# Row pitch in HBM: loads of 13,152 columns instead of 13,184 in a streaming Lp-pool kernel

## The chip, the cores and the metric

The kernel runs on one core of one Trainium2 chip. The metric is the device time of a run in microseconds, lower is better. Each quoted time is a median of several runs of the same kernel; all timed runs of this study were in the fast state (the one run of experiment e8 has an unknown state, because a single run has nothing to be compared with). A profile is one further execution.

## The reference

An Lp pool over windows of four with p = 2: for each group of four neighbouring values the root of the mean of their squares.

```python
x: float32 [32, 256, 4096], p = 2.0, kernel_size = 4
for i in range(1024):
    window = np.abs(x[:, :, 4*i:4*i+4]) ** p
    result[:, :, i] = np.mean(window, axis=-1) ** (1.0 / p)     # [32, 256, 1024]
```

134.2 MB come in and 33.6 MB go out. Windows never cross a row, so the kernel may treat x as one flat array.

## The kernel before

The flat array is cut into blocks of 128 rows, one row per partition of SBUF, the core's on-chip memory; HBM is the main memory that x and the result lie in. Two loads make a group: a block whose rows are two load widths long, and each load takes half of every row. So the row pitch in HBM is twice the load width, and the store's pitch is a quarter of that.

```python
W, O_W = 13184, 6592
X_SLOTS, O_SLOTS = 3, 2                       # three input buffers, two output buffers
slots = [[(W, [W])]] * 17 + [[(W, [6592, 6592])]]
slots += [[(6592, [6592]), (6592, [6592])], [(6592, [6592]), (4216, [2112, 2104])]]
ODD = 840                                     # the remainder, done first as 30 rows of 3584
groups = [2] * 9 + [3, 1]                     # loads to a group
late = {7, 8, 9, 10}                          # groups whose stores are issued after all loads
...
def block(flat, g, div):                      # group g of x (div = 1) or of the output (div = 4)
    at, width = sum(columns[:g]) * P // div, columns[g] * P // div
    return flat[at:at + width].rearrange("(p w) -> p w", p=P)

def load(i):
    ...
    nc.sync.dma_start(out=v, in_=block(xf, g, 1)[:, src:src + w])
...
def store(g, queue):
    stores[g] = queue.dma_start(out=block(of, g, k), in_=ots[g])
...
for i in range(n):                            # (cut) per load
    while ahead < n and loads[ahead][0] < s + X_SLOTS:
        load(ahead)                           # a load waits until its buffer's sums are done
        ahead += 1
    for step in chunks:
        nc.scalar.activation(out=v, in_=v, func=Act.Square)     # ScalarE, in place
        total_sum(ots[g][...], v, i)          # VectorE: a reduce over 4, or two adds (last 7 loads)
        while pending and pending[0][0] <= done - LAG:
            root(...)                         # ScalarE: Sqrt, then the group's store
for g in sorted(late):
    store(g, nc.sync)
```

## Time and profile before

| | before |
|---|---|
| time, median of 6 runs | 394.19 us (394.0 to 395.52) |
| span of the profiled run | 392.4 us |
| bytes moved | 167.77 MB, 428 GB/s over the span |
| busy: DMA engines / ScalarE / VectorE | 99.3% / 71% / 68% |
| load packet of 52,736 bytes: minimum / median | 1947 / 1947 ns |

The first row to read is the DMA share, because no compute engine is near full. The profile's lines for this table stand in the prediction below. A "packet" is one row of one partition; the 16 DMA engines have 16 of them in flight for 373 of the 392.4 us. Packet durations in this document come from the trace's records of single packets, of which the page shows only sums.

### The profile page before, as it was taken

Reading aid. Unit: us, or ns where it says so; the run is one execution under the profiler, and the core shown is the slowest. Engines: PE = TensorE matmul, PEld = TensorE weight load, DVE = VectorE, ACT = ScalarE, POOL = GpSimd, SP = SyncE. Lnnn points to the kernel's source line nnn. Section 1 sums busy time; section 2 is a strip of 40 time slices with the busy share of each in tenths; the row PEclk is TensorE's granted clock in tenths of the full one; section 3 lists DMA queues with packets and bytes.
Section 4 is the critical chain, followed back from the end, with each engine's and each line's share of the span. In section 5 each row is a group of like instructions: output and inputs, shape, how many; then the busy total and the mean of one; then the engine's idle time right before and its main releaser. Section 6 shows DMA issues by size and latency. Waiting matters only on the chain.

```text
span 392.4 us, 183 instructions
## 1 busy us (share of the span) xinstructions
DVE 268.5 (68%) x35; ACT 280.2 (71%) x39; POOL 0.2 (0%) x4
## 2 busy tenths in 40 slices
DVE  4307898885769476948693769396928690989481
ACT  1085879919990899099909990998099919999991
POOL 0000000000000000000000000000000000000000
DMA  8999999999999998999999999999999999999997
GB/s 318 425 441 430 446 441 441 411 435 470 430 398 430 473 430 387 430 473 430 411 441 438 430 473 425 392 430 430 430 435 452 446 430 446 409 430 416 446 430 321
DMA packets 4842, 167.77 MB, mean 428 GB/s; under 512 B 558, under 2 KB 558, under 8 KB 716
## 3 DMA queue, kind: packets, MB, share of 16 engines
q1 hardware_dynamic: 3789, 144.04, 85.3%
q10 hardware_dynamic: 1053, 23.73, 14.0%
HBM read 134.22 MB, written 33.55 MB: 428 GB/s over the span
## 4 chain that ended last, share of the span: by engine, by line
DMA 47%; ACT 34%; DVE 16%; SPq 0%; ACTq 0%; issue 0%
DMA xt<-in_x_dram 47%; ACT xt L162 28%; DVE ot L110 14%; ACT ot L101 6%; DVE xt L121 1%; DVE xt L123 1%; ACT xt L101 1%; ACTq L98 0%; SPq L81 0%; SPq L131 0%
## 5 line engine op out<-in xcount | busy, mean ns | idle before, releaser
L162 ACT ACTIVATE xt<-xt 128x13184 f32<-128x13184 f32 (+3 forms) x24 | 222.2, 9272 | 91.4 <-DMA xt<-in_x_dram 89.8
L110 DVE TENSOR_REDUCE ot<-xt 128x3296 f32<-128x13184 f32 x15 | 208.3, 13886 | 88.6 <-ACT xt L162 88.6
L101 ACT ACTIVATE ot<-ot 128x6592 f32<-128x6592 f32 x9 | 51.1, 5681 | 0.0
L121 DVE TENSOR_TENSOR xt<-xt 128x3296 f32<-128x3296 f32 (+3 forms) x9 | 34.5, 3836 | 22.5 <-ACT xt L162 22.2
L123 DVE TENSOR_TENSOR ot<-xt 128x3296 f32<-128x3296 f32 (+1 forms) x4 | 10.9, 2734 | 0.1
L142 ACT ACTIVATE ot<-ot 30x896 f32<-30x896 f32 x1 | 0.9, 948 | 10.9 <-DVE ot L138 10.9
L101 ACT ACTIVATE xt<-xt 128x3296 f32<-128x3296 f32 (+3 forms) x4 | 5.8, 1449 | 2.3 <-DVE xt L123 2.3
L136 DVE TENSOR_TENSOR ot<-ot 30x3584 f32<-30x3584 f32 x1 | 3.9, 3879 | 5.1 <-DMA ot<-in_x_dram 5.1
L123 DVE TENSOR_TENSOR xt<-xt 128x1648 f32<-128x1648 f32 (+2 forms) x5 | 7.0, 1407 | 0.2
L138 DVE TENSOR_REDUCE ot<-ot 30x896 f32<-30x3584 f32 x1 | 3.9, 3874 | 0.0
L142 ACT ACT_TABLE_LOAD x1 | 1.3, 1283 | 0.7 <-PEq L195 0.7
L195 POOL MEMSET const-bfloat16-1.0<- 128x1 bf16 x1 | 0.1, 101 | 0.0
L195 POOL MEMSET const-uint8-127<- 128x1 uint8 x1 | 0.1, 101 | 0.0
L195 POOL MEMSET const-float32-0.0<- 128x1 f32 x1 | 0.1, 98 | 0.2 <-issue 0.2
L195 POOL MEMSET const-float32-1.0<- 128x1 f32 x1 | 0.1, 98 | 0.0
## 6 DMA issues: line engine op xcount, KB each, us to landing
xt<-in_x_dram SPq DMA_DIRECT2D x18, 6592.0 KB, 31.3
out_dram<-ot ACTq DMA_DIRECT2D x7, 3296.0 KB, 27.0
xt<-in_x_dram SPq DMA_DIRECT2D x3, 3296.0 KB, 24.2
out_dram<-ot SPq DMA_DIRECT2D x2, 3296.0 KB, 26.2
out_dram<-xt SPq DMA_DIRECT2D x1, 2472.0 KB, 9.2
xt<-in_x_dram SPq DMA_DIRECT2D x1, 2108.0 KB, 23.7
out_dram<-xt SPq DMA_DIRECT2D x1, 527.0 KB, 5.9
ot<-in_x_dram SPq DMA_DIRECT2D x1, 420.0 KB, 4.3
```

The costliest lines, as they stand in the source:

```text
L101: r = nc.scalar.activation(out=o, in_=o, func=Act.Sqrt, scale=1.0 / k)
L110: r = nc.vector.tensor_reduce(out=o, in_=v.rearrange("p (n j) -> p n j", j=k), axis=mybir.AxisListType.X, op=add,)
L121: r = nc.vector.tensor_tensor(out=h, in0=q[:, :, 0:2], in1=q[:, :, 2:4], op=add)
L123: r = nc.vector.tensor_tensor(out=o, in0=h[:, :, 0], in1=h[:, :, 1], op=add)
L136: nc.vector.tensor_tensor(out=t, in0=t, in1=t, op=mybir.AluOpType.mult)
L138: nc.vector.tensor_reduce(out=o, in_=t.rearrange("p (n j) -> p n j", j=k), axis=mybir.AxisListType.X, op=mybir.AluOpType.add,)
L142: nc.scalar.activation(out=o, in_=o, func=Act.Sqrt, scale=1.0 / k)
L162: r = nc.scalar.activation(out=v, in_=v, func=Act.Square)
L195: nc = _bacc.Bacc("TRN2", target_bir_lowering=False, num_devices=1)
```

## The change

The intent: with rows of 105,472 bytes, rows four apart lie at the same place modulo 4 KB, since four rows are 103 x 4096 bytes. With 105,216 bytes they are 1 KB apart modulo 4 KB, which should spread the reads of the DMA engines in HBM.

```diff
-    W, O_W = 13184, 6592
+    W, O_W = 13152, 6576
-    slots = [[(W, [W])]] * 17 + [[(W, [6592, 6592])]]
-    slots += [[(6592, [6592]), (6592, [6592])], [(6592, [6592]), (4216, [2112, 2104])]]
+    slots = [[(W, [W])]] * 17 + [[(W, [6576, 6576])]]
+    slots += [[(6576, [6576]), (6576, [6576])], [(6576, [6576]), (4840, [3232, 1608])]]
-    in_x = {9: (2, 0), 10: (2, 4944)}
-    FINE, ENDS, LAG = {21}, {19, 20}, 1
+    in_x = {9: (2, 0), 10: (2, 4932)}
+    FINE, ENDS, LAGS = {21}, {19, 20}, {}
+    ON_DVE = set()
...
+            if (i, c) in ON_DVE:          # the set is empty: never taken
+                r = nc.vector.tensor_tensor(out=v, in0=v, in1=v, op=mybir.AluOpType.mult)
...
-            while pending and pending[0][0] <= done - LAG:
+            while pending and pending[0][0] <= done - LAGS.get(pending[0][1], 1):   # always 1
```

The last load grows from 4216 to 4840 columns, since it takes what the others leave.

More of the change, by code (lines that the diff above doesn't have):

```diff
@@ L161 @@
             v = xs[i][:, c:c + step]
-            r = nc.scalar.activation(out=v, in_=v, func=Act.Square)
-            follows(r, by_act[:-1])
-            by_act.append(r)
+            if (i, c) in ON_DVE:
+                r = nc.vector.tensor_tensor(out=v, in0=v, in1=v, op=mybir.AluOpType.mult)
+                follows(r, sums[:-1])
+            else:
+                r = nc.scalar.activation(out=v, in_=v, func=Act.Square)
+                follows(r, by_act[:-1])
+                by_act.append(r)
             total_sum(ots[g][:, summed:summed + step // k], v, i)
-            while pending and pending[0][0] <= done - LAG:
+            while pending and pending[0][0] <= done - LAGS.get(pending[0][1], 1):
                 root(*pending.pop(0)[1:])
```

## The prediction

> **What bounds the kernel now.** I read the page's slices first, because the kernel has no TensorE work and moves 167.8 MB.
>
> ```profile
> span 392.4 us, 183 instructions
> DVE 268.5 (68%) x35; ACT 280.2 (71%) x39; POOL 0.2 (0%) x4
> DMA  8999999999999998999999999999999999999997
> GB/s 318 425 441 430 446 441 441 411 435 470 430 398 430 473 430 387 430 473 430 411 441 438 430 473 425 392 430 430 430 435 452 446 430 446 409 430 416 446 430 321
> q1 hardware_dynamic: 3789, 144.04, 85.3%
> q10 hardware_dynamic: 1053, 23.73, 14.0%
> ```
>
> The compute engines are busy about 70% of the span, the DMA engines 85.3 + 14.0 = 99.3%. The rate wobbles by slice only because packets are long and are counted at their start. Wider stretches (length; DVE, ACT and POOL busy; clock; DMA share; GB/s) take the wobble away:
>
> ```profile
> 2.00:20.00 18.00, 7.75 (x2) 0.96 (x2) 0.00 (x0) 1.00 1.03 421
> 20.00:376.00 356.00, 253.42 (x28) 270.69 (x32) 0.00 (x0) 1.00 1.00 432
> 376.00:391.00 15.00, 7.28 (x6) 7.32 (x6) 0.00 (x0) 1.00 0.94 403
> ```
>
> From 20 to 376 us no DMA engine has time left. The chain of waits gives ScalarE and VectorE half of the path, which misleads here: the loads' queue waits for VectorE to free a slot, but it still has work queued.
>
> ```profile
> SPq L81 <- DVE ot L110: 301.6, 15, 43.2
> ...
> xt<-in_x_dram SPq DMA_DIRECT2D x18, 6592.0 KB, 31.3
> ```
>
> A 6.75 MB load needs 15.6 us at 432 GB/s, but takes 31.3 us from issue to landing: some 15 us of other traffic lies ahead of or between its packets. The issue therefore comes early enough.
>
> The question is then whether the engines move bytes as fast as they can, or whether their packets are drawn out by HBM, which is what the change wants to cure. I took the single packet records of the trace. Load packets of 52,736 bytes (one row of one partition; 2304 of them) take 1947 ns in the minimum, 1947 in the median, 1952 in the 90th percentile. The 1536 packets of 26,368 bytes (stores, and three half loads) take 978 in minimum and median. Two sizes give a line: (52,736 - 26,368) / (1947 - 978) = 27.21 bytes per ns and engine, plus 978 - 969 = 9 ns a packet. All the time above each size's median is 1.17 us per engine over the whole span, 0.54 of it in the first 20 us. Sum of the records by engine: first packet at 1.74 us, last end at 391.0 us[...]. So the 392.4 us are 1.74 us of start, 167.77 MB / 16 / 27.21 = 385.4 us of bytes, 4284 data packets / 16 x 9 ns = 2.4 us, 0.3 us of four-byte semaphore packets, 1.2 us of slow packets (sum 389.3), and 1.4 us of end.
>
> [...]
>
> **The change part by part.**
>
> Addresses. A group of two loads is one block of 128 rows of 2 x 13,184 x 4 = 105,472 bytes. Four rows are 421,888 = 103 x 4096[...]. With 13,152, four rows are 420,864 = 102.75 x 4096[...]. The kernel before holds its own control: the three half loads 18 to 20 form a group with rows of 79,104 bytes, four of which are 77.25 x 4096, also 1 KB apart, and stores of 26,368-byte rows are 1 KB apart too (25.75 x 4096). Both run at the same 978 ns, 8.6 ns above bytes / 27.2; the loads with equal addresses are 8.2 ns above. The spread buys nothing measurable there. Upper bound of what it can take away: the 1.17 us of slow packets. About 0.45 us of these are the first packets, drawn out while 16 engines start together, with the small first load of 30 partitions under way, which the change leaves; so I credit 0.3 us.
>
> Bytes and packets. The total is the same, to the byte: 32 columns fewer in 18 loads and 16 in each of three are 624 columns, and the last load grows from 4216 to 4840. The count of loads and stores stays, so 4284 data packets stay. A load packet becomes 52,608 / 27.21 + 9 = 1942 ns, a store packet 26,304 / 27.21 + 9 = 976 ns; the sums over bytes are equal. Change: 0.
>
> Alignment. 52,608 is 205.5 x 256, so each second load of a pair starts 128 bytes off; output rows of 26,304 bytes are 102.75 x 256.[...] But the 19,776-byte rows of group 9's store are 77.25 x 256 already, and take 735 ns where the line gives 736.[...]
>
> Compute. ScalarE squares 13,184 columns in 11.19 us and 6592 in 5.68, so 0.835 ns a column and 0.18 us fixed; VectorE's 13.89 us for a reduce shrinks by the same 0.24%. No instruction is added or removed. The squares on VectorE and the variable lag are switched off (an empty set, and a default of 1), so the order on every engine is unchanged. All of it lies beside the DMA.
>
> The tail. From 340.2 us ScalarE works without a pause of note until 385.6, so it could set the end:
>
> ```profile
> 373.92 2.95 ACT L101 ACTIVATE xt<-xt 128x3296 f32<-128x3296 f32 x1
> 376.78 1.95 ACT L162 ACTIVATE xt<-xt 128x2112 f32<-128x2112 f32 x1
> 379.51 1.58 ACT L101 ACTIVATE xt<-xt 128x1648 f32<-128x1648 f32 x1 [0.78 <-DVE xt L123]
> 381.11 4.88 SPq L98 DMA_DIRECT2D out_dram<-xt  x2
> ...
> out_dram<-xt SPq DMA_DIRECT2D x1, 2472.0 KB, 9.2
> ```
>
> Group 9's store is issued at 381.1 and lands 9.2 us later, while its 2.53 MB need 5.8 us at 432 GB/s: it stands 3.4 us behind the stores of groups 7 and 8. That is the slack of this chain. With the change load 17 lands some 0.7 us earlier (18 x 32 columns x 512 bytes = 0.29 MB at 432), seven squares and roots are 0.013 us shorter each, and the first chunk of the last load grows from 2112 to 3232 columns (2.88 us for 1.95, in place of the 0.78 us wait): 0.2 us later. Group 9's store comes about 0.6 us earlier. The last chunk falls to 1608 columns, its square to 1.52 us and the last roots to 0.85 and 0.52, so that the last store is issued near 384.1 instead of 385.6. It carries 0.62 MB instead of 0.54, taken from the stores before it. The queue empties at the same byte count: 0, with more slack.
>
> Sum: -0.3 + 0.3 + 0 + 0 = 0. The three runs before had 394.0, 395.49 and 395.52; their scatter is larger than anything in the sum. I put the new median between, at 394.9.
>
> **The rivals.** (a) The equal addresses do cost, in a way that packets hide. For it: 16 first packets at 2.2 to 2.9 us, and some 50 slow ones around 70 and 304 us just after a store was issued. Against it: their sum[...]. It would give 393.6 to 394.5, and cannot give more than 1.2 us. (b) The broken 256-byte alignment costs on both sides[...]. Against it: the 19,776-byte stores. (c) The tail turns bound to ScalarE: the larger first chunk would have to delay the store by 3.4 us more; it delays it by 0.2. Otherwise 396. (d) Smaller loads run the queue dry: impossible to see in a 0.24% change against 15 us queued ahead.
>
> **Range and chances.** A: 1.2 us down from the fastest seen before is 392.8[...]. The 2% lines are at 387.6 and 403.4. 387.6 less 1.8 us (394.2 for the profiled run, less its span) and 3.1 us of start and end leaves 382.7 us, less than the 385.4 us of bytes alone at 27.21[...]. Slower needs a new conflict of the spread addresses, which the control inside the trace speaks against. So 0.01, 0.97, 0.02.
>
> **What would show it.** Right: load packets near 1942 ns and store packets near 976, the share at 99%, 432 GB/s in the middle, the last store issued earlier but landed at the same time. If the first packets at 2 to 3 us fall to 1942, (a) is right in kind. If second loads or stores are over 10 ns above the line, (b). If the DMA share from 376 us on falls under 0.9, (c). Wrong outright: a middle rate above 435 or under 425 GB/s.

The sum came to 0: 0.3 us credited for the spread of addresses, 0.3 us charged for the lost alignment, 0 for compute and 0 for the tail. The charge, the upper bound of rival (b) and the upper end of the range, B, were worked out from a cost of a start off 256 bytes that was not shown; the charge stands in the line of the sum. 27.2 bytes per ns is, in the prediction or in an expectation, the measured 27.21, rounded.

## The result

394.49 us median of 6 runs (393.85 to 395.58), against 394.19 of before: the ratio is 1.0001, 95% interval 0.9977 to 1.0026, so the same. Here and below a ratio is the mean time of one kernel's runs over the mean of the other's runs of the same rounds, so it is not quite the ratio of the quoted medians.

The page of the changed kernel: its span, compute engines, the DMA's busy tenths and GB/s in 40 slices, and the two DMA queues (packets, MB, share).

```profile
span 392.3 us, 183 instructions
DVE 268.4 (68%) x35; ACT 280.2 (71%) x39; POOL 0.2 (0%) x4
DMA  8999999999989999999999999999999899999997
GB/s 307 433 436 429 445 445 461 394 434 469 434 386 429 472 429 413 461 413 429 429 429 429 429 472 429 429 432 459 429 440 429 386 432 469 405 443 417 444 432 321
q1 hardware_dynamic: 3789, 144.10, 85.3%
q10 hardware_dynamic: 1053, 23.68, 14.0%
```

Packets and shares are the same; 0.06 MB moved from the store queue to the load queue, because the earlier stores shrank. The three stretches of the changed kernel (length; DVE, ACT and POOL busy; clock; DMA share; GB/s):

```profile
2.00:20.00 18.00, 7.75 (x2) 0.96 (x2) 0.00 (x0) 1.00 0.99 407
20.00:376.00 356.00, 253.95 (x28) 271.19 (x33) 0.00 (x0) 1.00 1.00 433
376.00:391.00 15.00, 6.70 (x6) 6.83 (x5) 0.00 (x0) 1.00 0.96 406
```

The middle runs at 433 GB/s against 432. The 407 against 421 at the start is only where long packets happen to begin: the slow packets of that stretch cost 0.59 us per engine, against 0.53 before.

The load queue's wait for VectorE, from the changed kernel's waits, and the DMA table's time from issue to landing:

```profile
SPq L82 <- DVE ot L111: 300.7, 15, 43.3
...
xt<-in_x_dram SPq DMA_DIRECT2D x18, 6576.0 KB, 31.2
```

Both stand as before: long waits, and a load still finds some 15 us of traffic ahead of it, so the queue doesn't run dry, as the prediction's rival (d) would have it. The end of the changed kernel, from its timeline (start, duration; neighbours are merged, so the last line holds the stores of groups 9 and 10), and the landing time of group 9's store:

```profile
372.78 2.94 ACT L102 ACTIVATE xt<-xt 128x3288 f32<-128x3288 f32 x1
375.63 2.88 ACT L167 ACTIVATE xt<-xt 128x3232 f32<-128x3232 f32 x1
378.42 1.56 ACT L102 ACTIVATE xt<-xt 128x1644 f32<-128x1644 f32 x1
380.00 3.98 SPq L99 DMA_DIRECT2D out_dram<-xt  x2
...
out_dram<-xt SPq DMA_DIRECT2D x1, 2466.0 KB, 9.9
```

Group 9's store is issued 1.1 us earlier than before (380.00 against 381.11), takes 0.7 us longer to land, and the last packet ends at 390.9 us against 391.0. What compute gained, the queue took back. By packet: 52,608-byte loads have a minimum and a median of 1942 ns, 26,304-byte stores and half loads 975; the 90th percentile of the loads is 1942 too.

### The profile page after: what moved, and what is told of

The parts are those of the page before. It is cut to its first block, busy times and chain, and to the rows that moved or that the text cites. A ratio compares the mean times of both kernels' runs of the same rounds, so it can differ in the third digit from the quotient of the medians.

```text
span 392.3 us, 183 instructions
## 1 busy us (share of the span) xinstructions
DVE 268.4 (68%) x35; ACT 280.2 (71%) x39; POOL 0.2 (0%) x4
## 4 chain that ended last, share of the span: by engine, by line
DMA 47%; ACT 34%; DVE 15%; SPq 0%; ACTq 0%; issue 0%
DMA xt<-in_x_dram 47%; ACT xt L167 28%; DVE ot L111 14%; ACT ot L102 6%; ACT xt L102 1%; DVE xt L122 1%; DVE xt L124 0%; ACTq L99 0%; SPq L82 0%; SPq L132 0%
## 5 line engine op out<-in xcount | busy, mean ns | idle before, releaser
L167 ACT ACTIVATE xt<-xt 128x13152 f32<-128x13152 f32 (+3 forms) x24 | 222.2, 9272 | 90.9 <-DMA xt<-in_x_dram 89.2
L111 DVE TENSOR_REDUCE ot<-xt 128x3288 f32<-128x13152 f32 x15 | 207.8, 13853 | 88.2 <-ACT xt L167 88.2
L102 ACT ACTIVATE ot<-ot 128x6576 f32<-128x6576 f32 x9 | 51.0, 5669 | 0.0
L122 DVE TENSOR_TENSOR xt<-xt 128x3288 f32<-128x3288 f32 (+3 forms) x9 | 34.8, 3863 | 21.0 <-ACT xt L167 20.7
L124 DVE TENSOR_TENSOR ot<-xt 128x3288 f32<-128x3288 f32 (+1 forms) x4 | 10.9, 2726 | 0.1
L124 DVE TENSOR_TENSOR xt<-xt 128x1644 f32<-128x1644 f32 (+2 forms) x5 | 7.2, 1439 | 0.2
L102 ACT ACTIVATE xt<-xt 128x3288 f32<-128x3288 f32 (+3 forms) x4 | 5.9, 1479 | 0.8 <-DVE xt L124 0.8
```

The source lines that it names most:

```text
L102: r = nc.scalar.activation(out=o, in_=o, func=Act.Sqrt, scale=1.0 / k)
L111: r = nc.vector.tensor_reduce(out=o, in_=v.rearrange("p (n j) -> p n j", j=k), axis=mybir.AxisListType.X, op=add,)
L122: r = nc.vector.tensor_tensor(out=h, in0=q[:, :, 0:2], in1=q[:, :, 2:4], op=add)
L124: r = nc.vector.tensor_tensor(out=o, in0=h[:, :, 0], in1=h[:, :, 1], op=add)
L167: r = nc.scalar.activation(out=v, in_=v, func=Act.Square)
```

## The experiments

Theory: each DMA engine moves a packet in bytes / 27.21 + 9 ns, whatever the HBM address, so the time is set by bytes. Rivals: (a) the addresses matter but something hides it; (b) lost alignment eats a gain; (c) ScalarE's tail sets the end; and a fourth, from the page's chain: compute holds half the path. The runs were sent three times, four kernels each, and each time beside runs of the kernel before on the same chip: medians 394.42, 394.45 and 394.37 us. "Excess" is the time of load packets above their fast duration, summed and divided by 16 engines, in one profile.

### e1: the new kernel with the old row pitch

```diff
-        nc.sync.dma_start(out=v, in_=block(xf, g, 1)[:, src:src + w])
+        if g < 9:
+            first = sum(columns[:g]) * P + src
+            rows = xf[first:first + P * 26368].rearrange("(p w) -> p w", p=P)
+            nc.sync.dma_start(out=v, in_=rows[:, 0:w])
+        else:
+            nc.sync.dma_start(out=v, in_=block(xf, g, 1)[:, src:src + w])
```

> The changed kernel, but the loads of groups 0 to 8 read rows at the old pitch of 105,472 bytes[...], so only HBM read addresses differ; wrong result on purpose. Theory ([...]addresses modulo 4 KB don't matter): load packets stay at a median of 1942 ns, ratio to the kernel before 1.000 within 0.003, 394 to 395.5 us. Rival a (equal addresses cost, hidden in the changed kernel by a loss elsewhere): packets or first packets longer, 1 to 4 us slower than the changed kernel.

394.35 us, ratio 0.9989 (0.9973 to 1.0006); wrong result as intended. Load packets have a median and a 90th percentile of 1942 ns, and the excess is 1.0 us (0.8 in the changed kernel). With the addresses alone put back no loss is seen, so rival (a) fails as far as these runs can tell: the interval leaves room for about 1 us (0.3%), not for more.

### e2: the old kernel with the new row pitch

The same edit in the kernel before, with `P * 26304` in place of 26368.

> The kernel before with its own sizes, tail and 256-byte-aligned rows, but loads of groups 0 to 8 read rows at the new pitch of 105,216 bytes ([...]neighbouring rows overlap a little); wrong result on purpose. Theory: load packets at 1947 ns, ratio 1.000 within 0.003. Rival a: the spread alone gives the gain that the changed kernel's broken 256-byte alignment ate: 0.5 to 1.2 us less (ratio 0.997 to 0.999), slow packets gone.

395.45 us, ratio 1.001 (0.9992 to 1.0029), packets at 1947 ns. The spread alone buys nothing that shows either, so there was no gain for the alignment to eat.

The profile of this run shows one way in which the scatter of these kernels can arise. Its six runs are 394.25 once and 395.35 to 395.63 five times; the kernel before has the same two levels (six of its first runs: 394.0 to 394.3 four times, 395.5 twice), though single runs lie between (394.67 of the kernel before, 394.89 of the changed one). The profiled run fell in the upper level. The DMA's last 6 us (from 388 us on, 40 slices of 0.15 us) in e2:

```profile
DMA  9309993028999999931000000000000000000000
GB/s 396 132 0 396 1187 396 132 0 84 338 422 525 422 365 393 553 365 141 28 0 28 28 0 28 28 28 28 28 28 0 0 0 0 0 0 0 0 0 0 0
```

After the 141 the rate is 28 GB/s, that of one engine (27.21 bytes per ns by the line): the trace has eight packets of 4216 bytes one after the other, 0.16 us apart, ending at 392.42 us, when the other engines were done at about 391. Nine slow load packets between 154 and 246 us, of up to 2782 ns, are together 2.0 us above 1947 ns each, enough for one engine to fall behind. So a single late engine can set the end; why it fell behind stays open, and whether the upper level always comes from one isn't shown.

### e3 and e4: rows 128 KB and 1 MiB apart

e3 is e1 with 32,768 columns in place of 26,368. e4 takes x as 128 rows of 1 MiB:

```diff
-        nc.sync.dma_start(out=v, in_=block(xf, g, 1)[:, src:src + w])
+        at = sum(loads[j][2] for j in range(i))
+        rows = xf.rearrange("(p w) -> p w", p=P)
+        nc.sync.dma_start(out=v, in_=rows[:, at:at + w])
```

> The changed kernel with loads of groups 0 to 8 reading rows 131,072 bytes apart[...]; wrong result on purpose. Theory:[...] packets 1942 to 1960 ns, 394 to 397 us. Rival (HBM close to its limit, coinciding addresses hurt): load packets over 2100 ns and over 405 us.

> The changed kernel with all loads but the first small one reading rows exactly 1 MiB apart[...]; wrong result on purpose. The theory leaves this open, since it says only that 4 KB is harmless. If HBM has room at any address: 394 to 397 us. If rows a large power of two apart do collide: load packets lengthen by 10 to 30%, DMA rate in the middle under 400 GB/s, 420 to 490 us; then the cure of the change answers a real disease that this kernel did not have.

e3: 394.23 us, ratio 0.9987 (0.9969 to 1.0004), packets at 1942 ns, excess 0.76 us: all rows at equal places modulo 128 KB, and no cost that shows. e4: 404.78 us, ratio 1.025 (1.0224 to 1.0276). So rows 1 MiB apart do cost time; I had put its size too high (420 to 490 us, a guess that rested on no run). The median packet still takes 1942 ns, but the 90th percentile is 2221. The rate by stretch in e4 shows why it is small:

```profile
2.00:20.00 18.00, 7.75 (x2) 0.96 (x2) 0.00 (x0) 1.00 1.02 347
20.00:40.00 20.00, 4.59 (x1) 11.16 (x1) 0.00 (x0) 1.00 1.01 375
40.00:60.00 20.00, 15.44 (x2) 11.62 (x2) 0.00 (x0) 1.00 0.99 408
60.00:338.00 278.00, 198.35 (x16) 199.46 (x22) 0.00 (x0) 1.00 1.00 429
```

The same stretches of the changed kernel:

```profile
2.00:20.00 18.00, 7.75 (x2) 0.96 (x2) 0.00 (x0) 1.00 0.99 407
20.00:40.00 20.00, 8.03 (x1) 14.91 (x2) 0.00 (x0) 1.00 1.04 450
40.00:60.00 20.00, 18.38 (x2) 15.64 (x2) 0.00 (x0) 1.00 0.98 423
60.00:338.00 278.00, 197.06 (x17) 203.36 (x23) 0.00 (x0) 1.00 1.00 433
```

The DMA share is 1.0 in both: a slowed packet counts as busy, so only GB/s or the packets' durations show the loss. e4 loses at the start and then heals. Its excess is 9.86 us per engine, by 20 us: 3.46, 2.89, 1.03, 0.31, then seldom above 0.6.

### e12: does the store traffic heal it?

The first big store goes out at about the time when e4 has healed. e12 is e4 without the stores of groups 0 to 6.

```diff
-        if ends and g not in late:
+        if ends and g not in late and g > 6:
             store(g, nc.scalar)
```

> The kernel with loads 1 MiB apart, without the stores of groups 0 to 6 (left unwritten; wrong result on purpose): 23.6 MB less, so 54 us less by bytes. With 1 MiB the slow packets are nearly all in the first 60 us, and the first store is issued at 69. If the engines drift out of step by themselves: slow packets again end after about 60 us, some 10 us per engine in all, 349 to 354 us. If it is the stores in between that end them: slow packets go on through all loads (over 20 us per engine), 360 to 385 us.

348.83 us, just under the 349 to 354 expected; the excess by 20 us is 3.35, 2.45, 0.42, 0.13, and 9.1 us in all (later slices have up to 0.72). It heals without stores, so the stores aren't the cause.

That engines drift out of step is what is left of the two explanations, and the starts of the load packets speak for it. If all engines start together, there is a long pause between one bunch of starts and the next; if they are spread, all pauses are short. The longest pause between two starts in a row in e4 is 1.56 us from 10 to 20 us, 0.77 from 30 to 40 and 0.31 from 60 to 70; in e12 it is 1.63, 0.85 and 0.71. In e3, which has no such loss, it is still 1.03 us at 60 to 70 us: its engines stay bunched, and that costs nothing there. So the slow packets fade while the starts spread. That the one causes the other is an inference, since no run changes the spacing of starts alone.

### e10 and e11: the cure of the change, where the disease is

The pitch of e4 less 256 bytes (rows four apart are 1 KB apart modulo 4 KB, as in the change) and less 4 KB (all rows at equal places modulo 4 KB):

```diff
+        if g < 9:
+            at = sum(loads[j][2] for j in range(i))
+            rows = xf[0:P * 262080].rearrange("(p w) -> p w", p=P)     # e11: 261120
+            nc.sync.dma_start(out=v, in_=rows[:, at:at + w])
+        else:                                                          # as before
```

> The 1 MiB pitch of the run before it, less 256 bytes, for the loads of groups 0 to 8:[...] the very cure of the change, put where the disease was shown; wrong result on purpose. If the spread of 1 KB is a real cure: slow packets fall from 9.9 us per engine to about 1, first 20 us back near 408 to 436 GB/s, 394 to 396 us. If it isn't: 401 to 406 us as with the full 1 MiB.

> The same with 1 MiB less 4 KB[...]. If what collides at 1 MiB are places modulo 4 KB: no cure, 401 to 406 us. If it is coarser[...]: 394 to 396 us, slow packets about 1 us per engine. The theory takes the second, since equal places modulo 4 KB cost nothing at 103 KB and 128 KB pitch.

e10: 401.79 us, ratio 1.0184 (1.0153 to 1.0214), excess 5.0 us (90th percentile 2019 ns), first stretches at:

```profile
2.00:20.00 18.00, 7.75 (x2) 0.96 (x2) 0.00 (x0) 1.00 0.99 390
20.00:40.00 20.00, 6.82 (x1) 11.49 (x2) 0.00 (x0) 1.00 1.02 405
```

e11: 395.56 us, ratio 1.0023 (1.0003 to 1.0044), excess 1.5 us:

```profile
2.00:20.00 18.00, 7.75 (x2) 0.96 (x2) 0.00 (x0) 1.00 1.04 431
20.00:40.00 20.00, 8.17 (x1) 14.86 (x2) 0.00 (x0) 1.00 0.99 429
```

The 256 bytes halve the excess (9.86 to 5.0 us) and are not a cure: the time fits the second of my two forecasts for e10, the halving is in neither. The loss of time does not halve: it is 7.3 us over the kernel before, from 10.4 in e4 (medians of four runs on different chips, each beside its own runs of the kernel before). The excess is a mean over engines and leaves out late ones, which both profiles have: e10 has 16 packets in flight until 395.5 us, four at 396.0, and the last ends at 398.1; e4 has 16 until 399.9 us, and the last ends at 402.5.

Four KB of pitch is a cure as far as can be seen, although it leaves all rows equal modulo 4 KB: in the first 60 us the excess is 0.54 us, against 0.62 in the changed kernel. What is left of the time may be the scatter of e2, since the profiled run (395.57 us) has two packets in flight from 391.4 us on and ends its last at 392.4. The loss at 1 MiB is therefore not one of equal places modulo 4 KB (e3, with 394.23 us, had said so too), and the intent of the change names a period at which these runs show no cost. What collides at 1 MiB was not shown. In both kernels rows four apart are some 412 KB apart.

### e5: loads off every boundary

e1's edit with `+ src + 1` and the new kernel's own pitch: each load of groups 0 to 8 starts 4 bytes later. (The first of the two cases of the expectation: a cost for each such packet. These are 144 packets per engine.)

> The changed kernel, every load of groups 0 to 8 shifted by one column (4 bytes), so that no load packet starts on a boundary of 64 or 256 bytes; wrong result on purpose.[...] If alignment is free for packets of 50 KB: 1942 to 1944 ns and ratio within 0.003 of the changed kernel. Theory: the second, or a little over.

394.87 us, ratio 1.0007 (0.9982 to 1.0033), load packets 1942 ns in the median and the 90th percentile. A start 4 bytes off costs nothing that shows in a packet of 52,608 bytes. Rival (b) fails.

### e6: ScalarE at a third of its work

```diff
-                r = nc.scalar.activation(out=v, in_=v, func=Act.Square)
+                part = v[:, 0:step // 8]
+                r = nc.scalar.activation(out=part, in_=part, func=Act.Square)
```

and the roots become squares.

> The changed kernel with only the first eighth of each chunk squared (and the roots replaced by squares, so that no negative number meets a root); wrong result on purpose. ScalarE's busy time falls from 280 to about 95 us; DMA bytes are unchanged. Theory: bytes bind, 393.5 to 395.5 us. Rival (the chain of waits is right that ScalarE holds 34% of the path): over 5% faster, under 375 us.

394.19 us, ratio 0.999 (0.9971 to 1.001). The page of e6:

```profile
span 392.6 us, 197 instructions
DVE 268.1 (68%) x35; ACT 90.1 (23%) x39; POOL 0.2 (0%) x4
```

190 us of ScalarE's work gone, and no time. In the tail its last instruction ends at 373.8 us, ten earlier than in the changed kernel, and the last packet ends at 390.8 all the same. The 34% that the chain of waits gave ScalarE were no cost.

### e7: half of the store bytes

```diff
-        stores[g] = queue.dma_start(out=block(of, g, k), in_=ots[g])
+        part = columns[g] // k // 2
+        stores[g] = queue.dma_start(out=block(of, g, k)[:, 0:part], in_=ots[g][:, 0:part])
```

> The changed kernel storing only the first half of each row of every group's result (the rest of the output stays unwritten; wrong result on purpose): 16.7 MB less. Theory: 16.7 MB / 435 GB/s = 38.4 us less by bytes, 356 us; but the stores before load 17 lands then save only 27 us, and ScalarE's 45 us from load 17 to the end don't shrink, so the tail turns ScalarE-bound: 360 to 362 us. Rival (compute binds): under 10 us less.

360.13 us, 34.2 less than the kernel before. e7 by stretch:

```profile
20.00:320.00 300.00, 231.24 (x20) 242.22 (x27) 0.00 (x0) 1.00 1.00 432
320.00:340.00 20.00, 14.10 (x6) 20.00 (x5) 0.00 (x0) 1.00 1.01 433
340.00:350.00 10.00, 9.72 (x4) 10.00 (x4) 0.00 (x0) 1.00 0.87 368
350.00:358.00 8.00, 5.60 (x5) 5.69 (x5) 0.00 (x0) 1.00 0.39 157
```

Bytes bind until about 340 us; then ScalarE, busy throughout from 320 to 350, starves the DMA engines. The 38.4 us of bytes (at 435 GB/s, which is 16 x 27.21) give 34.2 us of time, as worked out before the run: the tail holds some 4 us of slack and then becomes the bound.

### e8: three loads on half of the engines

```diff
+        if i < 3:
+            for a in range(0, P, 32):
+                for b in range(a, a + 4):
+                    nc.sync.dma_start(out=v[b:a + 32:4], in_=block(xf, g, 1)[b:a + 32:4, src:src + w])
+        else:
             nc.sync.dma_start(out=v, in_=block(xf, g, 1)[:, src:src + w])
```

> The changed kernel with the first three loads cut into 16 DMAs of 8 partitions each (every fourth partition[...])[...]; right result. If each engine has its own limit of 27.2 bytes/ns: packets of those loads stay at 1942 ns or longer, 46 us more, near 441 us. If a common limit (HBM) sets the rate: packets shorten towards 970 ns and the time stays under 410 us. Theory: the first.

459.45 us (one run, right result). e8 by stretch:

```profile
5.00:85.00 80.00, 24.03 (x4) 23.27 (x3) 0.00 (x0) 1.00 0.49 207
92.00:108.00 16.00, 4.21 (x1) 0.00 (x0) 0.00 (x0) 1.00 1.06 224
115.00:400.00 285.00, 194.29 (x16) 208.82 (x23) 0.00 (x0) 1.00 1.00 430
```

The small DMAs have eight partitions each, and in the first stretch the trace has eight packets in flight at a time. They still take 1942 ns each, and the core moves 207 GB/s, half: the ceiling is one of each engine, not of HBM as a whole (all 16 move 430 GB/s from 115 us on). I had forecast 441 us; the second line shows the missing part. There all 16 engines are busy, yet the packets take 3941 ns in the median (3921 to 4107) and the sum is 224 GB/s. 16 packets at a time of 52,608 bytes in 3941 ns make 214 GB/s, near the 224. In that stretch the third load is still on its way (ScalarE waits for it until 113.72 us), and the first two whole-width loads are issued behind it (from 88.65 us on). Why packets take twice as long there was not shown: the profile names neither the engine of a packet nor its partition. Slow packets sum to 13.9 us per engine, of the 18 us missed; the rest was not followed.

### e9: the tail with one chunk

```diff
-[(6576, [6576]), (4840, [3232, 1608])]
+[(6576, [6576]), (4840, [4840])]
```

> The changed kernel with the last load taken in one chunk of 4840 columns instead of 3232 and 1608; right result. ScalarE is then 1.34 us longer before group 9's store is issued (near 381.3 us) and the last store is issued near 385.5 to 386 instead of 383.7. Theory (the end is set by bytes in the DMA engines, with over 3 us of slack in the chain of ScalarE): last packet still ends at 391 us within 0.3, 394 to 395.5 us. Rival c (ScalarE sets the end): 1.3 to 2 us later, 396 us and more.

394.66 us, ratio 1.001 (0.9984 to 1.0037), right result; last packet at 390.8 us. The two late stores of e9, and the landing time of group 9's:

```profile
381.29 4.28 SPq L99 DMA_DIRECT2D out_dram<-xt  x2
...
out_dram<-xt SPq DMA_DIRECT2D x1, 2466.0 KB, 8.5
```

Issued 1.29 us later than in the changed kernel, landed 1.4 us sooner after issue: the delay was slack in full. Rival (c) fails for the kernel as it is, and e7 shows where it would begin.

## Why the prediction was right

- **Bytes bind.** Confirmed both ways: e6 takes away 190 us of compute for no time, e7 takes away bytes and gains as computed until the tail binds. The issue-to-landing time of 31.3 us had said it before, against the chain of waits.
- **Packets already at the ceiling.** The line bytes / 27.21 + 9 ns gave 1942 ns and 976; measured 1942 and 975. That it holds "whatever the HBM address" is shown for the pitches of both kernels and for 128 KB; at 1 MiB it fails (e4). e8 adds that the ceiling holds for eight engines alone (1942 ns at 207 GB/s), so it isn't a shared HBM limit.
- **The spread.** The control in the kernel before was sound: e1 and e2 move only addresses, both within 0.2% of the kernel before (intervals within 0.3%). I had credited 0.3 us for the slow first packets; they didn't fall (2449 ns in the mean before, 2518 after). Excess in all fell from 0.97 to 0.80 us, too little for a claim from two profiles.
- **Alignment.** I charged 0.3 us; e5 and the packets show nothing (1942 ns with and without the shift). So neither the credit for the spread nor this charge came true. That they cancelled in the sum is luck, though both are smaller than the scatter.
- **The tail.** The direction and the slack were right, the shift was under-sized: load 17 landed 1.06 us earlier (squares begin at 339.16 us, 340.22 before), not 0.7, and group 9's store was issued 1.1 us earlier, not 0.6. Of the difference I had left out that seven stores of the earlier groups shrink too (7 x 16 columns x 512 bytes = 57 KB, 0.13 us at 432 GB/s) and that the excess differs by profile. None of it reaches the end.
- **Small readings.** Of the 1.17 us of slow packets, 0.66 lie in the first 20 us (0.53 for the large loads alone), not 0.54, and the 16 first packets make 0.50, not 0.45. A reading of gaps by engine is cut, since the trace names no engine; it does have at least 15 packets in flight at nearly all times from 4 to 389 us. The sum stands.
- **The end.** The sum took the mean over engines. e2 shows that the last engine counts: its late engine makes some 1.4 us in that profile, more than any term of the sum. The two levels of the times, 394 and 395.5, are in both kernels, and my 394.9 was put between them.

No version tried beats both. Bytes at the engines' rate are 385.4 of the 392.3 us of the span.

## What to carry to other kernels

Before curing HBM addresses, look at the durations of single packets: where the 90th percentile is within a few ns of the minimum (1952 and 1947 in the kernel before) and both lie on a line through bytes, there is little to cure. The median alone doesn't tell: it was 1942 ns in e4 too, which lost 10 us. A DMA share of 100% with a full GB/s figure (432 here) says the same in short. A busy DMA alone doesn't say it: with rows 1 MiB apart the share was 1.0 at 347 GB/s. With rows 1 MiB apart, 4 KB less pitch helped (395.56 us for 404.78), and 256 bytes less took off only some 3 of the 10 us lost (401.79). And where bytes bound, as here, ScalarE's 34% of the chain of waits was slack until the bytes shrank (e6, e7).
